# The low parts of one stage's weights, made a stage earlier and kept in DRAM

## The chip, the cores and the metric

One core of a Trainium2 chip runs the whole program. The metric is the time of one execution in device microseconds (us). TensorE (PE) multiplies, VectorE (DVE), ScalarE (ACT) and GpSimd (POOL) do the rest, and SyncE (SP) issues nearly all DMAs, in program order: a DMA that waits for a semaphore holds every DMA behind it on that engine.

## The reference

A trunk of two layers on 272 tokens (16 meta tokens and 256 of the input) of width 2048, in fp32. Each layer is a mixing part and a gated feed-forward; the mixing part of the second layer is an S5 scan beside an RWKV-7 recurrence:

```python
for layer in range(DEPTH):
    hn = rmsnorm(h, norm_mix_g[layer])
    if layer % 2 == 0:
        z = hn @ ev_w_in[j]          # LRU and differential attention
        ...
    else:
        z = hn @ od_w_in[j]          # 2048 x 4512
        u, dcols = z[..., :S5_WIDTH], z[..., S5_WIDTH:]
        yc = s5_layer(u, ...)        # then a gelu and a gated linear unit
        yd = rwkv7_time_mix(dcols, ...)
        mix = jnp.concatenate([yc, yd], axis=-1) @ od_w_out[j]
    h = h + mix
    h = h + swiglu(rmsnorm(h, norm_ffn_g[layer]), w_gate[layer], w_up[layer], w_down[layer])
```

## The kernel before

Activations lie with features on partitions and tokens along the row. Every dense product is exact to nearly fp32 by three passes: an operand is split into a high part that TensorE's fp32r format holds exactly and a low part, the rest, and `hi*xhi + hi*xlo + lo*xhi` is summed in PSUM (lines 193 to 195). A weight matrix is cut into pieces of 1024 x 128, 512 KB each. `load_piece_` loads a piece into `st`, casts it on ScalarE into `hi` (line 159) and subtracts on VectorE, `lo = st - hi` (line 160). `st`, `hi` and `lo` have three buffers each. A piece is 24 matmuls.

`run_dense` walks one list of items: the first mixing part, the first feed-forward (`ffn_items(0, ...)`), the second mixing part (`mix1_items`), the second feed-forward. An item is an output tile of 128 features: its pieces, where its input comes from, what to do with the result (`evac`), and what else to emit after it (`post`). Pieces are loaded a few ahead of use. `s5_setup` returns 15 steps that prepare tables for the S5 scan; they hang on every tenth item of the first feed-forward, the table steps at low priority, and the last one closes their pools. The tables go to DRAM (`s5p<-stb`, eight stores of 1088 KB) and come back as `stab` in the second mixing part.

In the second mixing part the items are the 36 tiles of `w_od_in`, two pieces each, in the order in which the scan (`s5_states`, from `us` and `stab`) and the recurrence (`rwkv`) need them; then the gated unit (`w_glu`) and the output product (`w_od_out`). `u` tiles are written to DRAM by `s5u<-zs` and `s5u<-ze` and read back as `us`. Scan and recurrence are long chains of small instructions over VectorE, ScalarE, GpSimd and TensorE. The order on each engine is made by the framework's scheduler when the program is built; priorities (`hi_pri` for weight loads) move instructions forward in it.

Of the kernel before, what the change touches and what calls it, by code (L numbers as in the profile page):

```python
# [9 lines left out]
F32 = mybir.dt.float32  # L10
F32R = mybir.dt.float32r
AF = mybir.ActivationFunctionType
ALU = mybir.AluOpType
# [81 lines left out]
class Net:  # L95
# [50 lines left out]
    def lo_pri(self):  # L146
        return self.tc.high_priority(offset=-1000000)

    def load_piece(self, ap, kc):
        with self.hi_pri():  # L150
            return self.load_piece_(ap, kc)

    def load_piece_(self, ap, kc):
        nc = self.nc
        st = self.t(self.wst, [128, 8, 128], "st")
        nc.sync.dma_start(st[:, :kc], ap)
        hi = self.t(self.whi, [128, 8, 128], "hi", F32R)
        lo = self.t(self.wlo, [128, 8, 128], "lo", F32R)
        nc.scalar.copy(hi[:, :kc], st[:, :kc])  # L159
        nc.vector.tensor_tensor(lo[:, :kc], st[:, :kc], hi[:, :kc].bitcast(F32), op=ALU.subtract)  # L160
        return hi, lo

    def run_dense(self, items, first=(), lead=0, ahead=2):

        nc = self.nc
        flat = [(i, j) for j in range(2) for i in range(lead)]
        flat += [(i, j) for i, it in enumerate(items) for j in range(len(it["pieces"])) if i >= lead]
        loads = [x for x in flat if items[x[0]]["pieces"][x[1]]]
        ready = dict(zip(loads, first))
        banks, done = {}, {}  # L170
        nxt, pos = len(first), 0
        for i, j in flat:
            it = items[i]
            if j == 0:
                if it.get("pre"):
                    it["pre"]()
                banks[i] = self.ps(it["bank"]) if "bank" in it else self.pd.tile([128, 512], F32, tag="p", name="p")
                done[i] = 0
            if it["pieces"][j]:
                while nxt < min(pos + 1 + ahead, len(loads)):  # L180
                    ready[loads[nxt]] = self.load_piece(*items[loads[nxt][0]]["pieces"][loads[nxt][1]])
                    nxt += 1
                pos += 1
                hi, lo = ready.pop((i, j))
            a, b, k0, c0, n = it["x"]()
            kc = it.get("kc") or it["pieces"][j][1]
            o = it.get("off", 0)
            tot = it.get("kc") or sum(kc for _, kc in it["pieces"])
            p = banks[i]
            for k in range(kc):  # L190
                kk = done[i]
                xa, xb = a[:, k0 + kk, c0:c0 + n], b[:, k0 + kk, c0:c0 + n]
                nc.tensor.matmul(p[:, :n], hi[:, o + k], xa, start=kk == 0, stop=False)  # L193
                nc.tensor.matmul(p[:, :n], hi[:, o + k], xb, start=False, stop=False)  # L194
                nc.tensor.matmul(p[:, :n], lo[:, o + k], xa, start=False, stop=kk == tot - 1)  # L195
                done[i] += 1
            if done[i] == tot:
                it["evac"](p[:, :n])
                if it.get("post"):
                    it["post"]()  # L200
# [385 lines left out]
    def s5_setup(self):  # L586

        nc = self.nc
# [3 lines left out]
        es = ExitStack()  # L592
        st = {}
# [100 lines left out]
        def weights_b():  # L694

            pl = st["plq"]
            bb = st["bb"]
            hm = self.s5c["hq"]
            eh = self.t(pl, [128, 8, 2, 2, 64], "seh", F32R)
            el = self.t(pl, [128, 8, 2, 2, 64], "sel", F32R)  # L700
            for g in range(2):
                m = hm[:, g:g + 1]
                nc.scalar.activation(eh[:, :, :, g], bb, AF.Copy, scale=m)
                V.scalar_tensor_tensor(el[:, :, :, g], bb, m, eh[:, :, :, g].bitcast(F32), op0=M, op1=S)
            par = self.s5_par.rearrange("(c s) p w -> s p c w", s=4)
            for i, x in enumerate((eh, eh, el, el)):
                for sc in range(4):
                    nc.sync.dma_start(par[sc, 32 * i:32 * i + 32, :, 2 * T:2 * T + 256],
                                      x[32 * sc:32 * sc + 32].rearrange("p c m g s -> p c (m g s)").bitcast(F32))
            st["es2"].close()  # L710
            st["pl2"] = self.pool("s5s2", 2, es)

        def weights_c(half):
            def f():
                cw = self.t(st["pl"], [128, 16, 3, 2, 16], "scw")
                for i, m in ((0, 0), (1, 1), (2, 1)):
                    for g in range(2):
                        sg = self.base["hm"][:, g:g + 1] if i < 2 else self.s5c["hn"][:, g:g + 1]
                        nc.scalar.activation(cw[:, :, i, g], st["c"][:, m, 16 * half:16 * half + 16], AF.Copy, scale=sg)
                nc.sync.dma_start(self.s5_par[16 * half:16 * half + 16, :, 2 * T + 256:].rearrange("j p c -> p j c"),  # L720
                                  cw.rearrange("p a i g c -> p a (i g c)"))
            return f
# [38 lines left out]
        def low(fn):  # L761
            def f():
                with self.lo_pri():
                    fn()
            return f

        steps = [scalars, factors, weights_b, weights_c(0), weights_c(1), small]
        steps += [low(table(g)) for g in range(8)]
        steps.append(es.close)
        return steps  # L770

    def s5_states(self, c, u, sc):
# [50 lines left out]
    def mix1_items(self):  # L823
        nc = self.nc
        I = self.I
        st = {}
        w, wo, wg = I["w_od_in"], I["w_od_out"], I["w_glu"]
        items = []
# [96 lines left out]
        def outp(last, m):  # L925
            def evac(p):
                self.add_h(p, m, NM)
                if last:
                    self.norm_chunk(m, "g_ffn1", NM)
                    if m == KC - 1:  # L930
                        st["es"].close()
            return evac

        def add(m, evac):
            items.append(dict(pieces=[(w[m, j], 8) for j in range(2)], x=x_in, evac=evac))

        for m, n in ((32, "w"), (33, "a"), (34, "g0"), (35, "g1")):
            add(m, lora(n, m - 8))
        add(0, u(0))
        for pr in range(8):  # L940
            for i in range(3):
                e = 3 * pr + i
                for c in range(1, 8):
                    if (4 * c * S5E + 31) // 32 - 1 == e:
                        add(c, u(c))
                add(8 + 8 * i + pr, rkv(pr, i))
# [13 lines left out]
        for m in range(KC):  # L960
            items.append(dict(pieces=[None if m % nb else (self.I["w_od_last"][m // nb], 8)], 
                              x=lambda: (*st["yd"], 0, 0, TR), kc=8 - YA, off=m % nb * (8 - YA), evac=outp(True, m)))
# [244 lines left out]
    def build(self, upto=99):  # L1207
        nc = self.nc
        with self.es:
            self.setup()  # L1210
            items = self.mix0_items()
            first = []
            with self.tc.high_priority(offset=100000):
                nc.sync.dma_start(self.vec, self.I["vec"])
            items[0].pop("pre")()
            with self.tc.high_priority(offset=100000):
                for a, b, i in ((0, 2, 1), (2, 8, 2), (8, 16, 0)):
                    nc.sync.dma_start(self.h[:, a:b], self.I["hT"][:, a:b])
                    for _ in range(i):
                        first.append(self.load_piece_(*items[len(first)]["pieces"][0]))  # L1220
                self.base = self.load_const("base", self.cp)
                self.mhalf = self.t(self.cp, [128, 8], "mhalf")
                nc.vector.memset(self.mhalf, -0.5)
                self.attn_setup()
                for k in range(KC):
                    self.norm_split(k, "g_mix0", 0)
            for k in range(KC):
                self.norm_square(k, 0, True)
            f0 = self.ffn_items(0, 0, None, lambda m: self.norm_chunk(m, "g_mix1", 0))
            steps = self.s5_setup()  # L1230
            for i, fn in enumerate(steps):
                f0[2 + 10 * i]["post"] = fn
            items += f0
            if upto > 1:
                items += self.mix1_items()
            if upto > 2:
                items += self.ffn_items(1, NM, None, self.final)
            self.run_dense(items, first, 3)
            if upto > 2:
                self.output()  # L1240
            if "h" in self.dbg:
                nc.sync.dma_start(self.dbg["h"], self.h)
# [95 lines left out]
```

## Time and profile before

| | |
|---|---|
| median of 3 runs | 2631.05 us (2630.87 to 2631.34) |
| the profiled execution | 2625.82 us, span 2624.0 us |
| TensorE busy | 2558.7 us, 98% of the span |
| VectorE, ScalarE, GpSimd busy | 1698.1, 1221.0, 591.2 us |
| mean granted TensorE clock | 0.989 of full speed |
| DMA | 448.37 MB, mean 171 GB/s |

The profile is one execution. Busy time is the time in which an engine executes; TensorE's is modelled and counts overlapping matmuls once. Positions are us from the start of the span: the first feed-forward runs from about 430 to 1225, the second mixing part to about 1850. The granted clock is the share of full TensorE speed (2.4 GHz) in a stretch; its lower level is 1.2 GHz.

### The profile page before, as it was taken

How to read it: one execution, taken by the hardware profiler on the slowest of the kernel's cores; microseconds unless marked ns; L12 is line 12 of the kernel's file. 1: busy time of each engine (PE TensorE's matmuls, PEld its weight loads, DVE VectorE, ACT ScalarE, POOL GpSimd, SP SyncE). 2: the span in 40 equal slices, each digit the busy share in tenths (PEclk: the TensorE clock that was granted, in tenths of full speed). 3: DMA queues.
4: the chain of work that ended last, by engine and by line, in shares of the span. 5: the costliest groups of instructions: out<-in, count | busy, mean ns of one | idle time of the engine just before them, and what ended most of it. 6: DMA issues, size and time to landing. Idle time of an engine off the chain costs nothing. (4 is left out here: it accounts for less than half of the span.)

```text
span 2624.0 us, 50534 instructions
## 1 busy us (share of the span) xinstructions
PE 2558.7 (98%) x20072; PEld 2467.8 (94%) x20072; DVE 1698.1 (65%) x2700; ACT 1221.0 (47%) x2111; POOL 591.2 (23%) x820
## 2 busy tenths in 40 slices
PE   8999999999999999999999999999999999999998
PEld 7999999999999999999877788899999999999997
DVE  7666768787555555557688898765655555555555
ACT  5555546488334333335334444554544434343434
POOL 3111312100001010102276777630210101010103
PEclk9999999999999999999999999999999999999999
DMA  5444456767655555555554444233555555555554
GB/s 193 145 141 139 145 180 199 223 221 243 204 176 176 172 176 175 172 176 180 176 163 150 140 143 128 87 117 124 175 186 179 187 186 185 188 185 185 185 185 145
DMA packets 160317, 448.37 MB, mean 171 GB/s; under 512 B 35089, under 2 KB 51153, under 8 KB 159825
## 3 DMA queue, kind: packets, MB, share of 16 engines
q1 hardware_dynamic: 143504, 442.84, 52.0%
q10 hardware_dynamic: 16576, 2.30, 0.5%
q8 instruction: 159, 2.61, 0.4%
q14 instruction: 78, 0.63, 0.1%
HBM read 422.20 MB, written 22.87 MB: 170 GB/s over the span
## 5 line engine op out<-in xcount | busy, mean ns | idle before, releaser
L159 ACT CAST hi<-st 128x1024 fp32r<-128x1024 f32 (+1 forms) x776 | 792.9, 1022 | 1074.5 <-PE p L194 770.0
L160 DVE TENSOR_TENSOR lo<-st,hi 128x1024 fp32r<-128x1024 f32 (+1 forms) x776 | 936.4, 1207 | 489.8 <-ACT hi L159 485.8
L193 PE MATMUL p<-xhi,hi 128*128 128x272 f32 (+1 forms) x4256 | 1233.5, 290 | 12.4 <-ACT hi L159 10.0
L195 PE MATMUL p<-xhi,lo 128*128 128x272 f32 (+1 forms) x4256 | 1236.5, 291 | 7.0 <-DVE lo L160 6.9
L194 PE MATMUL p<-xlo,hi 128*128 128x272 f32 (+1 forms) x4256 | 1229.6, 289 | 0.0
L193 PEld LDWEIGHTS p<-xhi,hi 128*128 128x128 f32 x4256 | 809.1, 190 | 25.7 <-issue 12.9
L195 PEld LDWEIGHTS p<-xhi,lo 128*128 128x128 f32 x4256 | 809.0, 190 | 20.8 <-issue 11.2
L194 PEld LDWEIGHTS p<-xlo,hi 128*128 128x128 f32 x4256 | 807.6, 190 | 10.8 <-issue 10.0
L299 POOL TENSOR_TENSOR ga<-ga,rb 128x272 f32<-128x272 f32 (+1 forms) x88 | 126.1, 1433 | 1231.5 <-ACT ga L298 1231.5
L195 PE MATMUL p<-ah,lo 128*128 128x272 f32 (+1 forms) x1408 | 401.9, 285 | 0.4 <-DVE lo L160 0.4
L193 PE MATMUL p<-ah,hi 128*128 128x272 f32 (+1 forms) x1408 | 401.0, 285 | 0.3 <-ACT hi L159 0.3
L194 PE MATMUL p<-al,hi 128*128 128x272 f32 (+1 forms) x1408 | 400.9, 285 | 0.0
L195 PEld LDWEIGHTS p<-ah,lo 128*128 128x128 f32 x1408 | 265.8, 189 | 0.7 <-DVE lo L160 0.7
L193 PEld LDWEIGHTS p<-ah,hi 128*128 128x128 f32 x1408 | 265.6, 189 | 0.6 <-ACT hi L159 0.6
L194 PEld LDWEIGHTS p<-al,hi 128*128 128x128 f32 x1408 | 264.8, 188 | 0.0
L208 DVE TENSOR_TENSOR h<-p,h 128x256 f32<-128x256 f32 (+1 forms) x272 | 116.8, 430 | 145.1 <-PE p L195 144.1
L245 POOL TENSOR_TENSOR acc<-acc,sq 128x272 f32<-128x272 f32 (+1 forms) x56 | 60.7, 1084 | 260.0 <-ACT sq L240 259.5
L308 DVE TENSOR_TENSOR gu<-p,ga 128x272 f32<-128x272 f32 (+1 forms) x88 | 38.1, 433 | 62.4 <-PE p L195 59.9
L297 DVE TENSOR_TENSOR ga<-p,rb 128x272 f32<-128x272 f32 (+1 forms) x88 | 38.0, 432 | 53.4 <-PE p L195 52.8
L806 POOL TENSOR_TENSOR sx<-stab,sz 128x256 f32<-128x256 f32 x64 | 63.5, 995 | 27.6 <-DVE sz L803 10.5
L1096 POOL TENSOR_TENSOR xt<-ls,xs 40x15 f32<-40x15 f32 (+7 forms) x120 | 49.9, 416 | 43.8 <-DMA ls<-ld 37.4
L218 DVE SCALAR_TENSOR_TENSOR xlo<-h,vec,xhi 128x272 fp32r<-128x272 f32 (+1 forms) x64 | 50.7, 800 | 0.6 <-ACT xhi L217 0.5
(383 smaller groups left out, 2594.4 us busy)
## 6 DMA issues: line engine op xcount, KB each, us to landing
st<-in_w_gate SPq DMA_DIRECT2D x176, 512.0 KB
st<-in_w_up SPq DMA_DIRECT2D x176, 512.0 KB
st<-in_w_down SPq DMA_DIRECT2D x160, 512.0 KB
st<-in_w_ev_in SPq DMA_DIRECT2D x80, 512.0 KB
st<-in_w_od_in SPq DMA_DIRECT2D x72, 512.0 KB
st<-in_w_ev_out SPq DMA_DIRECT2D x32, 512.0 KB
stab<-s5p SPq DMA_DIRECT2D x32, 448.0 KB
s5p<-stb SPq DMA_DIRECT2D x8, 1088.0 KB
```

The source lines that it names most:

```text
L159: nc.scalar.copy(hi[:, :kc], st[:, :kc])
L160: nc.vector.tensor_tensor(lo[:, :kc], st[:, :kc], hi[:, :kc].bitcast(F32), op=ALU.subtract)
L193: nc.tensor.matmul(p[:, :n], hi[:, o + k], xa, start=kk == 0, stop=False)
L194: nc.tensor.matmul(p[:, :n], hi[:, o + k], xb, start=False, stop=False)
L195: nc.tensor.matmul(p[:, :n], lo[:, o + k], xa, start=False, stop=kk == tot - 1)
L208: self.nc.vector.tensor_tensor(self.h[:, m, c0:], p, self.h[:, m, c0:], op=ALU.add)
L218: nc.vector.scalar_tensor_tensor(lo, src, g, hi.bitcast(F32), op0=ALU.mult, op1=ALU.subtract)
L245: nc.gpsimd.tensor_tensor(self.acc[:, c0:], self.acc[:, c0:], sq[:, c0:], op=ALU.add)
L299: nc.gpsimd.tensor_tensor(a[:, :n], a[:, :n], self.rb[:, :n], op=ALU.mult)
L308: nc.vector.tensor_tensor(u[:, :n], p, a[:, :n], op=ALU.mult)
L806: (V if i == 3 else G).tensor_tensor(pr[i], a[:, NM:], b[:, NM:], op=M)
L1096: G.tensor_tensor(o, ls[:, s + 1:, s].unsqueeze(1).to_broadcast([40, j, n]), xs[:, :j, s:s + 1].to_broadcast([40, j, n]), op=M)
```

## The change

The low parts of the 72 pieces of `w_od_in` are no longer made when the pieces are used. A new function `park` loads a piece into `pst`, casts it into `phi`, subtracts in place and stores the result to a DRAM tensor `od_lo`; 72 calls of it hang on items of the first feed-forward from item 24 on, spread evenly by pieces. In the second mixing part such a piece's `hi` is cast as before, and its `lo` is loaded from DRAM. The S5 pools are closed near the end of the feed-forward instead of at item 142, since the two double-buffered tiles of `park` live among them. The scratch space that the framework keeps for dynamic DMAs is set to 1024.

```diff
-    def load_piece_(self, ap, kc):
+    def load_piece_(self, ap, kc, parked=None):
...
         nc.scalar.copy(hi[:, :kc], st[:, :kc])
-        nc.vector.tensor_tensor(lo[:, :kc], st[:, :kc], hi[:, :kc].bitcast(F32), op=ALU.subtract)
+        if parked is None:
+            nc.vector.tensor_tensor(lo[:, :kc], st[:, :kc], hi[:, :kc].bitcast(F32), op=ALU.subtract)
+        else:
+            nc.sync.dma_start(lo.bitcast(F32), parked)
         return hi, lo
+
+    def park(self, pl, ap, parked):
+        nc = self.nc
+        st = self.t(pl, [128, 8, 128], "pst")
+        nc.sync.dma_start(st, ap)
+        hi = self.t(pl, [128, 8, 128], "phi", F32R)
+        nc.scalar.copy(hi, st)
+        nc.vector.tensor_tensor(st, st, hi.bitcast(F32), op=ALU.subtract)
+        nc.sync.dma_start(parked, st)
...
             st["pl2"] = self.pool("s5s2", 2, es)
+            self.park_pool = self.pool("park", 2, es)
...
-            items.append(dict(pieces=[(w[m, j], 8) for j in range(2)], x=x_in, evac=evac))
+            items.append(dict(pieces=[(w[m, j], 8, self.od_lo[m, j]) for j in range(2)], x=x_in, evac=evac))
...
+            first_, todo, at = 24, list(parts), 0.0
+            each = sum(size[first_:-4]) / len(parts)
+            for i in range(first_, len(f0) - 4):
+                at += size[i]
+                while todo and at >= each:
+                    at -= each
+                    posts[i].append(lambda x=todo.pop(0): self.park(self.park_pool, x[0], x[2]))
...
+            posts[-2].append(lambda: self.s5_pools.close())
...
-    nc = bacc.Bacc("TRN2", target_bir_lowering=False, num_devices=1)
+    nc = bacc.Bacc("TRN2", target_bir_lowering=False, num_devices=1, dynamic_dma_scratch_size=1024)
```

The scheduler places what this emits. Three places are shown, each before and after; line numbers of the changed program are its own (its 156 is the weight load, 161 the subtraction, 163 the load of `lo`, 170 to 174 the park).

SP in the first feed-forward, between its gate and up products and the down product of a slice. Before, there are weight loads alone:

```order
L156 DMA st<-in_w_gate 128x1024 x2
L156 DMA st<-in_w_up 128x1024 x2
L156 DMA st<-in_w_gate 128x1024 x2
L156 DMA st<-in_w_up 128x1024 x2
L156 DMA st<-in_w_down 128x1024 x32
```

After, with the semaphores that each row waits for (`DVE_49` is VectorE's, `DMAHWn_49` those of earlier DMAs, which is how a park's load waits for the store that frees its buffer):

```order
L156 DMA st<-in_w_gate 128x1024 [waits DMAHW5_49,DVE_49]
L170 DMA pst<-in_w_od_in 128x1024 [waits DMAHW3_49,DMAHW0_49]
L156 DMA st<-in_w_up 128x1024 [waits DMAHW6_49,DVE_49]
L174 DMA odlo<-pst 128x1024 [waits DVE_49]
L156 DMA st<-in_w_up 128x1024 [waits DMAHW1_49,DVE_49]
L156 DMA st<-in_w_down 128x1024 [waits DMAHW7_49,DMAHW2_49,DVE_49]
L170 DMA pst<-in_w_od_in 128x1024 [waits DMAHW5_49]
L174 DMA odlo<-pst 128x1024 [waits DVE_49]
L156 DMA st<-in_w_down 128x1024 [waits DMAHW4_49,DVE_49]
L156 DMA st<-in_w_down 128x1024 [waits DMAHW6_49,DMAHW3_49,DVE_49]
```

For every two or three weight loads there is now one park's load and one store, each with a wait of its own. All 72 stand between the 145th and the 314th weight load of the program.

SP at the start of the second mixing part. Before (the first rows of its weight loads):

```order
L156 DMA st<-in_w_od_in 128x1024 [waits DMAHW6_49,DVE_49]
L156 DMA st<-in_w_od_in 128x1024 [waits DMAHW7_49,DVE_49]
L133 DMA c_rw<-in_c_rw 128x912 [waits PE_49]
L978 DMA lw<-in_w_lora 128x256 [waits Pool_49]
L980 DMA lg<-in_w_lora 128x256
L156 DMA st<-in_w_od_in 128x1024 [waits DMAHW0_49,DVE_49]
```

After:

```order
L163 DMA lo<-odlo 128x1024 [waits PE_49]
L156 DMA st<-in_w_od_in 128x1024 [waits DMAHW6_49,Activation_49]
L163 DMA lo<-odlo 128x1024 [waits PE_49]
L156 DMA st<-in_w_od_in 128x1024 [waits DMAHW7_49,Activation_49]
L163 DMA lo<-odlo 128x1024 [waits PE_49]
L133 DMA c_rw<-in_c_rw 128x912
L994 DMA lw<-in_w_lora 128x256 [waits Pool_49]
L156 DMA st<-in_w_od_in 128x1024 [waits DMAHW0_49,Activation_49]
```

Weight loads and `lo` loads now alternate. A `lo` load waits for TensorE to release the buffer (`PE_49`), a weight load for the cast (`Activation_49`) instead of the subtraction.

VectorE inside the second mixing part, where scan (`sx`, `sz`, `sp`), recurrence (`rkv`, `lz`) and weights share it. Before:

```order
L802 SCALAR_TENSOR_TENSOR sz_15205<-s_rho,sx_15191 128x272
L160 TENSOR_TENSOR lo<-st,hi 128x1024
L806 TENSOR_TENSOR sp_15212<-stab,sz_15205 128x256
L803 SCALAR_TENSOR_TENSOR sz_15206<-s_rho,sx_15192 128x272
L1059 TENSOR_TENSOR lz<-a,c_rw 128x64
L1059 TENSOR_TENSOR lz<-a,c_rw 128x2x64
L792 TENSOR_TENSOR sx_15302<-c,stab 128x272
L793 TENSOR_TENSOR sx_15303<-c,stab 128x272
L204 TENSOR_TENSOR zs<-p,rb 128x272
L160 TENSOR_TENSOR lo<-st,hi 128x1024
```

After:

```order
L816 SCALAR_TENSOR_TENSOR sz_15753<-s_rho,sx_15739 128x272
L820 TENSOR_TENSOR sp_15760<-stab,sz_15753 128x256
L1048 TENSOR_TENSOR ri_14967<-rkv_16225,rcu 128x4x64
L817 SCALAR_TENSOR_TENSOR sz_15754<-s_rho,sx_15740 128x272
L217 TENSOR_TENSOR zs<-p,rb 128x272
L806 TENSOR_TENSOR sx_15773<-c,stab 128x272
L807 TENSOR_TENSOR sx_15774<-c,stab 128x272
```

The subtractions of input weights are gone from between the scans; the rest stands in a new order. On TensorE the first matmul that reads `us` (line 791) comes 325 dense matmuls after the last one of the norm's broadcast (line 269), where it came after 248.

## Rows read from the trace of the kernel before

**Rows 1.** The page's first lines: span, and busy time by engine.

```profile
span 2624.0 us, 50534 instructions
PE 2558.7 (98%) x20072; PEld 2467.8 (94%) x20072; DVE 1698.1 (65%) x2700; ACT 1221.0 (47%) x2111; POOL 591.2 (23%) x820
```

**Rows 2.** Busy time by stretch, with clock and DMA.

```profile
core 0: us, PE busy (x) PEld busy (x) DVE busy (x) ACT busy (x) POOL busy (x), PEclk, DMA share, GB/s
1260.00:1290.00 30.00, 25.95 (x184) 25.76 (x183) 15.98 (x24) 8.39 (x10) 5.25 (x9) 0.89 0.56 175
1290.00:1640.00 350.00, 337.62 (x2285) 278.39 (x2283) 294.87 (x464) 149.77 (x308) 249.12 (x425) 0.99 0.47 147
1640.00:1730.00 90.00, 82.34 (x611) 73.28 (x610) 67.19 (x123) 49.20 (x115) 54.08 (x100) 0.96 0.30 91
440.00:700.00 260.00, 252.38 (x1950) 250.12 (x1949) 194.04 (x358) 162.05 (x387) 25.64 (x21) 0.98 0.68 222
700.00:1200.00 500.00, 500.00 (x3967) 500.00 (x3967) 266.43 (x312) 193.19 (x224) 39.58 (x28) 1.00 0.53 174
```

**Rows 3.** Waits of TensorE, 1260 to 1730: us in total, times, longest.

```profile
PE a L1202 <- DVE re L1199: 5.9, 4, 2.4
PE d L807 <- POOL sx L806: 4.1, 3, 2.8
PE c L791 <- DMA us<-s5u: 4.0, 1, 4.0
PE e L1157 <- DVE w L1154: 2.4, 1, 2.4
...
```

**Rows 4.** Timeline around one gap: start, us, engine, line, instruction.

```profile
1364.06 1.19 DVE L160 TENSOR_TENSOR lo<-st,hi 128x1024 fp32r<-128x1024 f32 x1
1365.18 0.95 DVE L1199 COPY re<-iv 68x512 f32<-68x512 f32 x1
...
1366.28 0.30 PE L1202 MATMUL a<-c_base,re 68*128 68x68 f32 x1 [2.45 <-DVE re L1199]
```

**Rows 5.** Chain of waits, 1260 to 1730: the subtractions before 1640 on it.

```profile
1511.87 1.58 DVE lo L160
...
1533.61 1.19 DVE lo L160
...
1611.84 1.21 DVE lo L160
```

**Rows 6.** Line 160 from 1260 to 1730: min, median and max ns.

```profile
L160 DVE TENSOR_TENSOR lo<-st,hi x72: 1191/1224/1808, 1259.7 to 1726.0; 128x1024 fp32r<-128x1024 f32 x72
```

**Rows 7.** Line 156 from 1250 to 1800: the loads of `w_od_in`.

```profile
L156 SPq DMA_DIRECT2D st<-in_w_od_in x61: 327/333/634, 1251.9 to 1623.5; - x61
```

**Rows 8.** Waits of ScalarE, 700 to 1200; the 166 casts there.

```profile
ACT hi L159 <- PE p L194: 221.4, 113, 2.0
ACT hi L159 <- issue: 84.8, 52, 1.9
...
L159 ACT CAST hi<-st x166: 1047/1051/1053, 699.8 to 1199.1; 128x1024 fp32r<-128x1024 f32 x166
```

**Rows 9.** Waits of SP, 700 to 1200.

```profile
SPq L156 <- DVE lo L160: 368.9, 141, 2.9
```

**Rows 10.** Timeline of SP and ScalarE from 593: loads issued, casts that waited.

```profile
593.40 1.32 SPq L156 DMA_DIRECT2D st<-in_w_gate  x2
595.39 4.16 SPq L156 DMA_DIRECT2D st<-in_w_up  x2
...
596.88 1.05 ACT L159 CAST hi<-st 128x1024 fp32r<-128x1024 f32 x1 [0.47 <-DMA st<-in_w_gate]
599.26 1.05 ACT L159 CAST hi<-st 128x1024 fp32r<-128x1024 f32 x1 [0.50 <-DMA st<-in_w_gate]
601.88 1.05 ACT L159 CAST hi<-st 128x1024 fp32r<-128x1024 f32 x1 [1.57 <-DMA st<-in_w_up]
```

**Rows 11.** Timeline: a table's store, and what waited for it.

```profile
585.04 0.43 SPq L757 DMA_DIRECT2D s5p<-stb  x1
...
590.61 0.30 DVE L747 COPY stb<-stq 128x256 f32<-128x256 f32 x1 [0.77 <-DMA s5p<-stb]
```

**Rows 12.** Timeline of TensorE: the first matmul that reads `us`.

```profile
1276.98 0.57 PE L791 MATMUL c<-us,stab 128*128 128x272 f32 x1 [4.05 <-DMA us<-s5u]
```

**Rows 13.** The page's DMA lines: queue, packets, MB, share; issues.

```profile
q1 hardware_dynamic: 143504, 442.84, 52.0%
...
st<-in_w_od_in SPq DMA_DIRECT2D x72, 512.0 KB
...
s5p<-stb SPq DMA_DIRECT2D x8, 1088.0 KB
```

**Rows 14.** Busy time in one microsecond.

```profile
604.00:605.00 1.00, 1.00 (x11) 1.00 (x10) 0.82 (x4) 1.00 (x3) 0.00 (x0) 1.00 1.06 418
```

More of the change, by code (lines that the diff above doesn't have):

```diff
@@ L147, in lo_pri, with load_piece @@
         return self.tc.high_priority(offset=-1000000)
-    def load_piece(self, ap, kc):
+    def load_piece(self, *piece):
         with self.hi_pri():
-            return self.load_piece_(ap, kc)
-    def load_piece_(self, ap, kc):
+            return self.load_piece_(*piece)
+    def load_piece_(self, ap, kc, parked=None):
         nc = self.nc
@@ L187, in run_dense @@
             o = it.get("off", 0)
-            tot = it.get("kc") or sum(kc for _, kc in it["pieces"])
+            tot = it.get("kc") or sum(x[1] for x in it["pieces"])
             p = banks[i]
@@ L765, in low @@
             return f
+        self.s5_pools = es
         steps = [scalars, factors, weights_b, weights_c(0), weights_c(1), small]
         steps += [low(table(g)) for g in range(8)]
-        steps.append(es.close)
         return steps
@@ L932, in outp @@
             return evac
+        self.od_lo = self.dr.tile([36, 2, 128, 8, 128], F32, tag="odlo", name="odlo")
         def add(m, evac):
-            items.append(dict(pieces=[(w[m, j], 8) for j in range(2)], x=x_in, evac=evac))
+            items.append(dict(pieces=[(w[m, j], 8, self.od_lo[m, j]) for j in range(2)], x=x_in, evac=evac))
         for m, n in ((32, "w"), (33, "a"), (34, "g0"), (35, "g1")):
@@ L1229, in build @@
             f0 = self.ffn_items(0, 0, None, lambda m: self.norm_chunk(m, "g_mix1", 0))
-            steps = self.s5_setup()
-            for i, fn in enumerate(steps):
-                f0[2 + 10 * i]["post"] = fn
+            m1 = self.mix1_items()
+            posts = [[] for _ in f0]
+            for i, fn in enumerate(self.s5_setup()):
+                posts[2 + 10 * i].append(fn)
+            parts = [x for it in m1 for x in it["pieces"] if x and len(x) == 3]
+            size = [sum(x[1] for x in it["pieces"]) for it in f0]
+            first_, todo, at = 24, list(parts), 0.0
[5 more added lines that the diff above has]
+                    posts[i].append(lambda x=todo.pop(0): self.park(self.park_pool, x[0], x[2]))
+            for x in todo:
+                posts[-5].append(lambda x=x: self.park(self.park_pool, x[0], x[2]))
+            posts[-2].append(lambda: self.s5_pools.close())
+            for it, fns in zip(f0, posts):
+                if fns:
+                    it["post"] = lambda fns=fns: [f() for f in fns]
             items += f0
-            if upto > 1:
-                items += self.mix1_items()
+            items += m1
             if upto > 2:
```

## The prediction

> **What bounds the kernel now.** I read the page first, then busy time by stage, then who TensorE waited for. The profiled execution took 2625.82 us around a span of 2624.0 us; the median of the runs is 2631.05, so every difference worked out below in the profile's microseconds is put on 2631.05, and the 0.2% between the two is passed over. TensorE is busy 2558.7 us of the span [rows 1]: what can be won is the 65 us in which it is idle, and what its clock loses after such a gap. By stage [rows 2] the reader should see three different kernels. In the first feed-forward from 700 to 1200 us TensorE has 500 of 500 us, VectorE 266 and ScalarE 193: nothing there can be won, and there is room to hide work. From 440 to 700 us, where the feed-forward shares its engines with the preparation of the S5 tables, TensorE is idle 7.6 us and VectorE and ScalarE are fuller (194 and 162 of 260). In the second mixing stage TensorE is idle 4.05 us in 1260 to 1290, 12.38 in 1290 to 1640 and 7.66 in 1640 to 1730, and VectorE is the fullest of the others, 294.87 of 350 us (84%). The granted clock of these three stretches is 0.89, 0.99 and 0.96 of full speed; the missing share is worth 3.3, 3.5 and 3.6 us at 2.4 GHz.
>
> The waits [rows 3] name VectorE or GpSimd behind most of this idle time, and one DMA: the first `us` load, 4.0 us. One gap shows the mechanism that the change aims at [rows 4]: TensorE waits 2.45 us for `re` of line 1199, and VectorE had run a 1.19 us subtraction of line 160 right before it. In the chain of waits the subtraction of input weights stands three times with 1.58, 1.19 and 1.21 us [rows 5]. That chain reaches back only to 1487 us.
>
> **The change, part by part.** (1) *Removed.* 72 subtractions go from VectorE in the second mixing stage. One takes 1.22 us [rows 6], so 88 us in all, some 66 of them in 1290 to 1640, where VectorE falls from 84% to about 65%. What that gives TensorE lies between 1.1 us (the one gap of [rows 4], in which the subtraction stood directly ahead) and 12.4 us (all idle time of 1290 to 1640; the last of these 72 pieces is loaded at 1623.5, [rows 7]). The nearest row is the chain: 3.98 us in the 153 us from 1487 to 1640, so 9.9 us over the 380 us from 1260. I take 10, and of the 3.5 us that the clock loses there the same share, 3.
>
> (2) *A moved start.* The order shows that in the new program 325 dense matmuls instead of 248 stand between the last matmul of the norm (line 269) and the first that needs `us`. At 0.126 us each (500 us for 3967 [rows 2]) this is 9.7 us more time for that load. Bounds: nothing, if the load is late by as much, since the new `lo` loads stand in the same queue; 7.3 us, if the gap and its clock loss both go (4.05 + 3.3). I take 4.
>
> (3) *Added in the first feed-forward*, 72 times: a 512 KB load, a ScalarE cast of 1.05 us, a VectorE subtraction of 1.22 us and a 512 KB store. Casts and subtractions come to 76 and 88 us. The cover is the slack of 700 to 1200 us: ScalarE waits there for TensorE to release `hi` [rows 8], 306 us over 166 casts, 1.8 us in each period of 3.02 us (24 matmuls of 0.126), and VectorE is 53% busy. Engine time costs nothing there. Without that cover, as in part of 440 to 700 us, a park is 2.3 us on the way to the next `hi` and `lo`.
>
> The queue is the doubtful part. SP issues in order. Before, it sits in front of each weight load waiting for VectorE, 369 us over 141 loads, 2.6 us of 3.02 [rows 9]. Now a store that waits for its subtraction, or a park load that waits until its buffer's store has landed, holds the weight loads behind it, and those hold TensorE. By the order, 170 weight loads (154 of 512 KB, 16 of 256 KB) stand between the first park's load and the last one's store: 162 periods of 3.02 us, 490 us, so a park every 6.8 us and, with two buffers, 13.6 us for one round of load, cast, subtraction and store. What a round needs: a 512 KB load lands 3.5 us after issue when it is alone (593.40 to 596.88) and 4.9 us when one is ahead [rows 10]; a cast waits up to 2.0 us for its turn behind a `hi` cast and takes 1.05, the subtraction 1.22 and up to as much for its turn; the store takes 3.5 us if like a load, 5.6 if like the `stb` store of 1088 KB (585.04 to 590.61) [rows 11]. Low end 9.3, high end 16.0, middle 12.6 us. With 12.6 the rounds fit, tightly. I take 4 us for moments where they don't, above all before 700 us; bounds 0 and 85 us ((16.0 - 13.6) / 2 times 72).
>
> (4) *Added in the second mixing stage:* 72 loads of 512 KB into `lo`. A `lo` load can be issued when TensorE has finished the piece three before, two pieces ahead of its use. In the first 20 pieces hardly anything stands between the dense matmuls, so that is 6.05 us; later, 380 us for some 60 pieces makes it about 12.6. A load with two others in flight lands after 6.5 us (595.39 to 601.88) [rows 10], so in the long run it is in time, and in the first 20 pieces it may be late by up to 0.44 us, 9 us in all. The `s5u` stores, the first of which holds `us` back until 1276.98 [rows 3, 12], stand in the same queue and can add to it. I take 4 us; bounds 0 and 61 (a landing of 9.1 us, one more transfer of 2.6 us ahead, is late by 3.0 in each of 20 pieces).
>
> (5) *Moved and freed.* The S5 pools are closed at the end of the feed-forward instead of at its item 142; what takes their place begins only after that feed-forward, so this costs nothing. In the mixing stage an `st` buffer is now free after the cast, 1.2 us earlier than after the subtraction: nothing won, since the weight loads have been early enough there (of the waits of [rows 3] none is for `st`). The smaller scratch space carries no instruction of the profile.
>
> The sum: -10 - 3 - 4 + 0 + 4 + 4 = -9 us, from 2631 to **2622 us**.
>
> **The rivals.** *No difference.* In 1290 to 1640 TensorE is 96% busy; if the gaps only move to the next late engine (GpSimd is at 71%, 249 of 350), the gain is the 1.1 us of the one gap, or what is won is given back in (3) and (4). For it: the waits in [rows 3] run through GpSimd's `iv` and `sx` as well as VectorE. Time 2626 to 2636.
>
> *The parks become the bound of the feed-forward* (the other side). Transfers in that stretch: 154 x 512 + 16 x 256 KB of weights, 72 x 1024 KB of parks and 8 x 1088 KB of tables, 169.3 MB in 490 us, 345 GB/s. Over the whole span queue 1 moved 442.84 MB in 52.0% of the time of 16 engines [rows 13], which is 325 GB/s at full occupancy. At that rate the stretch takes 522 us: +32. With the gains and the cost of (4), -13, it gives 2650; if rounds of 16.0 us decide, +85 and 2703. Against it: with a store and a load in flight together, single microseconds show 418 GB/s [rows 14], and sustained at that rate 405 us would do. It decides from a round of 13.6 us, or below 345 GB/s. The Trainium skill (DMA: Bandwidth & Descriptors, section Specifications) gives a limit of about 358 GB/s of HBM for one core and 435 GB/s for the engines. By the former the 169.3 MB would take 473 us, so this rival would cost nothing on average. The rate of [rows 14] is beyond 358, so the trace does not bear that limit out for single microseconds, and no row shows 345 held for 490 us.
>
> *`lo` comes late at the start of the mixing stage.* If a landing takes 7.0 us in place of 6.05, 20 pieces lose 19 us, against gains of 17 and the 4 us of (3): 2637. It speaks for it that the same stretch asks for 1 MB every 3.02 us, 347 GB/s, with the `s5u` stores between.
>
> *More than forecast.* All idle time of 1290 to 1730 outside the DMA gap goes (20.0), the clock follows (7.1) and so does the first gap (7.3), at no cost: -34, 2597.
>
> **How the numbers follow.** The forecast, 2610 to 2625, has 0.40; more than that, down to 2597, 0.12; no difference 0.19; the parks as bound 0.16; late `lo` 0.13. A measurement of this kernel can tell about 0.2% (5.3 us) from no change. Faster by more than that takes the first two, 0.52; within it 0.19; slower 0.29. The range leaves out the far half of the parks' rival and little at the low end: 2597 to 2655. Without the two slower cases it would be 2600 to 2633.
>
> **What would show it.** Right: in the stretch that is now 1290 to 1640, VectorE near 65% busy, TensorE's idle time near 3 us, no wait of line 195's matmuls for a DMA named `lo<-odlo` beyond the first 20 pieces, and 500 of 500 us busy in the feed-forward with DMA at some 345 GB/s. Wrong: ScalarE waiting for `st` or `pst` loads in the feed-forward and TensorE idle behind `hi`, with the clock below 1.00 there (the parks); TensorE waiting for `odlo` (late `lo`); or the same idle time in the mixing stage with other releasers, GpSimd first (no difference).

## The result, and the profile after

The changed kernel takes 2650.91 us (median of 5 runs, 2644.98 to 2657.92) against 2631.05 before: ratio 1.0074, 95% interval 1.0052 to 1.0095. It is slower by 20 us, where 9 us faster was forecast. The time lies within the range and on the other side of no change; it is the time that the rival "the parks become the bound of the feed-forward" gave (2650). The profiled execution took 2652.13 us.

The page of the kernel after, its first lines and its chain of waits, to be read beside [rows 1]:

```profile
span 2650.3 us, 50949 instructions
PE 2568.2 (97%) x20072; PEld 2471.8 (93%) x20072; DVE 1688.5 (64%) x2700; ACT 1293.3 (49%) x2183; POOL 552.5 (21%) x820
...
PE 71%; DMA 14%; DVE 6%; issue 3%; ACT 3%; POOL 2%; SPq 1%; ACTq 0%; DVEq 0%; POOLq 0%
```

The totals say little: all engines have about the work they had, ScalarE 72 us more. Only the chain of waits (third line) points somewhere: DMA has 14% of it. The stretches, with the columns of [rows 2], say where:

```profile
440.00:700.00 260.00, 239.79 (x1788) 233.76 (x1787) 208.34 (x371) 175.42 (x399) 27.32 (x17) 0.97 0.85 297
700.00:1200.00 500.00, 495.48 (x3901) 492.37 (x3900) 309.05 (x350) 236.84 (x264) 37.57 (x28) 1.00 0.81 277
...
1290.00:1670.00 380.00, 367.17 (x2527) 311.31 (x2525) 236.43 (x422) 163.04 (x325) 218.95 (x446) 0.97 0.71 234
1670.00:1760.00 90.00, 84.31 (x600) 73.51 (x600) 69.13 (x126) 47.24 (x113) 55.62 (x103) 0.96 0.29 83
```

The number behind each x counts matmuls, and in the feed-forward all are alike, so the difference to [rows 2] is TensorE's lag, idle time and slow clock together. From 440 to 700 us there are 1788 in place of 1950, 162 fewer, 20.4 us at 0.126 us each. From 700 to 1200 there are 3901 in place of 3967, 66 fewer, 8.3 us. That makes 28.7 us lost in the first feed-forward. The issue of the first mixing piece's load agrees, 1216.59 us before and 1246.92 after, 30.3 us later.

The mixing stage does get its VectorE relief: 236 of 380 us (62%) in 1290 to 1670, where it was 84%. TensorE gets little of it. Over 700 us of that stage it is idle 29.0 us before (1200 to 1900, busy 671.02) and 25.2 after (1230 to 1930, busy 674.82).

Waits of ScalarE, 500 to 1250 us, in the kernel after (us in total, times, longest):

```profile
ACT hi L159 <- PE p L207: 122.9, 76, 2.0
ACT phi L172 <- DMA pst<-in_w_od_in: 84.6, 43, 4.0
ACT hi L159 <- issue: 28.6, 18, 1.7
ACT hi L159 <- DMA st<-in_w_down: 25.0, 22, 3.1
ACT hi L159 <- DMA st<-in_w_gate: 23.2, 24, 2.2
```

Waits of SP in the same stretch:

```profile
SPq L156 <- DVE lo L161: 256.4, 134, 3.5
SPq L170 <- DMA odlo<-pst: 107.1, 52, 4.6
...
SPq L174 <- DVE pst L173: 39.3, 37, 5.0
```

Before, ScalarE waited there for TensorE and had time in hand [rows 8]. Now it waits for weights on their way, and 43 times for a parking load at the head of its own order. SP stands 107 us before parking loads until the buffer's store has landed. TensorE's own waits, 440 to 700 us, are for weights (in the kernel before they were 3.4 and 4.1 us in the same stretch):

```profile
PE p L206 <- ACT hi L159: 10.9, 8, 3.4
PE p L208 <- DVE lo L161: 9.1, 11, 2.5
```

This is what the prediction named as the sign of the rival. The waits show two candidates and not which of them costs the time: too many bytes, or waiting instructions at the head of an order.

### The profile page after: what moved, and what is told of

The parts are those of the page before. It is cut to its first block, busy times and chain, and to the rows that moved or that the text cites. A ratio compares the mean times of both kernels' runs of the same rounds, so it can differ in the third digit from the quotient of the medians.

```text
span 2650.3 us, 50949 instructions
## 1 busy us (share of the span) xinstructions
PE 2568.2 (97%) x20072; PEld 2471.8 (93%) x20072; DVE 1688.5 (64%) x2700; ACT 1293.3 (49%) x2183; POOL 552.5 (21%) x820
## 4 chain that ended last, share of the span: by engine, by line
PE 71%; DMA 14%; DVE 6%; issue 3%; ACT 3%; POOL 2%; SPq 1%; ACTq 0%; DVEq 0%; POOLq 0%
PE p L208 21%; PE p L206 21%; PE p L207 21%; DMA odlo<-pst 5%; DMA pst<-in_w_od_in 4%; PE d L821 2%; DVE lo L161 2%; DMA st<-in_w_gate 1%; DMA lo<-odlo 1%; ACT hi L159 1%; DVE pst L173 1%; ACT phi L172 1%; DMA st<-in_w_down 1%; PE b L1139 1%; POOL xs L1114 1%
## 5 line engine op out<-in xcount | busy, mean ns | idle before, releaser
L161 DVE TENSOR_TENSOR lo<-st,hi 128x1024 fp32r<-128x1024 f32 (+1 forms) x704 | 842.7, 1198 | 410.3 <-ACT hi L159 404.1
L173 DVE TENSOR_TENSOR pst<-pst,phi 128x1024 f32<-128x1024 f32 x72 | 89.1, 1237 | 69.2 <-ACT phi L172 67.8
L172 ACT CAST phi<-pst 128x1024 fp32r<-128x1024 f32 x72 | 75.4, 1047 | 85.1 <-DMA pst<-in_w_od_in 84.6
L820 POOL TENSOR_TENSOR sx<-stab,sz 128x256 f32<-128x256 f32 x64 | 54.6, 855 | 28.8 <-DVE sz L817 11.1
```

The costliest lines, as they stand in the source:

```text
L172: nc.scalar.copy(hi, st)
L173: nc.vector.tensor_tensor(st, st, hi.bitcast(F32), op=ALU.subtract)
L820: (V if i == 3 else G).tensor_tensor(pr[i], a[:, NM:], b[:, NM:], op=M)
```

## The experiments

"Lag" is the matmuls missing against [rows 2] in 440 to 700 and in 700 to 1200 us, times 0.126 us. "Rest" is the difference of the medians less both lags: what the other stages, mostly the mixing stage, win (-) or lose. The lags come from one profiled execution each, in which some matmul records can be missing, and the late parks still run after 1200 us; the three kernels without loads in the mixing stage have rests of 4.2, -0.7 and 2.8, so a rest is good to some 4 us. Each kernel was timed beside the kernel before on the same chip (medians 2630.38, 2629.42 and 2630.02 in the three groups of four).

| kernel | median us | ratio (95%) | lag 440–700 | lag 700–1200 | rest |
|---|---|---|---|---|---|
| changed kernel | 2650.91 | 1.0074 (1.0052–1.0095) | 20.4 | 8.3 | -8.8 |
| parks only | 2657.94 | 1.0101 (1.0086–1.0117) | 18.5 | 4.9 | 4.2 |
| loads only | 2617.96 | 0.9949 (0.9934–0.9965) | -2.0 | 0 | -10.4 |
| parks, transfers only | 2660.36 | 1.0119 (1.0101–1.0137) | 26.7 | 4.0 | -0.7 |
| parks, engines only | 2635.27 | 1.0020 (1.0008–1.0031) | 2.1 | 0 | 2.8 |
| paced | 2634.77 | 1.0019 (1.0006–1.0033) | 3.4 | 9.3 | -7.4 |
| paced, late | 2644.19 | 1.0055 (1.0037–1.0073) | -1.8 | 18.8 | -2.2 |
| parks on GpSimd's queue | 2681.45 | 1.0198 (1.0179–1.0218) | 26.1 | 27.6 | -1.7 |
| paced, late, four `lo` | 2657.86 | 1.0104 (1.0086–1.0122) | -2.4 | 19.4 | 11.4 |
| staged, late | 2625.31 | 0.9990 (0.9980–1.0000) | -0.8 | 1.1 | -5.0 |
| half of the parks | 2634.46 | 1.0025 (1.0012–1.0038) | 15.8 | 0 | -11.4 |
| staged | 2623.56 | 0.9980 (0.9971–0.9988) | 3.2 | 0 | -9.7 |
| staged, late, half | 2618.30 | 0.9961 (0.9948–0.9974) | -1.1 | 0 | -10.6 |

**Which half of the change costs.** Parks only: the mixing stage keeps its subtractions.

```diff
-        if parked is None:
+        if True:
             nc.vector.tensor_tensor(lo[:, :kc], st[:, :kc], hi[:, :kc].bitcast(F32), op=ALU.subtract)
```

> The 72 parks of the first feed-forward are as in the changed kernel, but the mixing stage computes its low parts by subtraction as before, and nothing reads what was parked. If the loss lies in the first feed-forward (theory A, from the trace of after: first mixing piece reached 30 us later, the stage itself only 3 us shorter), this costs 26 to 32 us over the kernel before, about 2660, and is slower than the changed kernel by about 3 to 10. If the loss came from the stage that loads the parked parts (theory B), it is within 6 us of before, 2631 to 2637.

Loads only: one piece is parked, and all 72 loads read that place.

```diff
-                    posts[i].append(lambda x=todo.pop(0): self.park(self.park_pool, x[0], x[2]))
+                    x = todo.pop(0)
+                    if x is parts[0]:
+                        posts[i].append(lambda x=x: self.park(self.park_pool, x[0], x[2]))
...
-            nc.sync.dma_start(lo.bitcast(F32), parked)
+            nc.sync.dma_start(lo.bitcast(F32), self.od_lo[32, 0])
```

> One piece is parked, and all 72 low parts of the mixing stage are loaded from that one place, so the low parts are not the reference's. This is the mixing stage of the changed kernel without the traffic in the feed-forward. Theory A: 3 to 13 us faster than before, 2618 to 2628 (13 is what the prediction gave this stage, 3 is what the trace of after shows). Theory B: 20 us or more slower than before.

2657.94 and 2617.96: theory A twice (the second at the edge of its range), B falls. Parking costs 27.6 us, loading wins 12.4. Together they give +15.2, and the changed kernel has +19.9, with an interval of 13.7 to 25.0 us: the difference is within the noise.

**Transfers or engine work.** Both keep the subtractions of the mixing stage. Transfers only, in `park`:

```diff
-        hi = self.t(pl, [128, 8, 128], "phi", F32R)
-        nc.scalar.copy(hi, st)
-        nc.vector.tensor_tensor(st, st, hi.bitcast(F32), op=ALU.subtract)
```

> Parks without cast and subtraction: each piece is loaded and stored again as it is, and the mixing stage subtracts as before. A1 (the feed-forward loses because its transfers need more than the roughly 325 GB/s that the DMA moves at full occupancy): nearly all the loss stays, 20 to 30 us over before, about 2656. A2 (it loses because parking casts and subtractions stand in ScalarE's and VectorE's order waiting for the parking load, and hold up the weights' casts behind them): under 8 us over before, 2631 to 2639.

Engines only, in `park`, where `st` is one tile that is set once:

```diff
-        nc.sync.dma_start(st, ap)
...
-        nc.sync.dma_start(parked, st)
```

> Parks without transfers: the 72 casts and 72 subtractions run on one tile that is in place, and the mixing stage subtracts as before. A1: within 4 us of before, 2628 to 2636. A2: the same, since nothing waits. A3 (the loss is the engine time itself, 150 us of ScalarE and VectorE together, most of it at 550 to 660 us where both engines are already at 42 of 50 us): 10 to 25 us over before, 2641 to 2656.

2660.36 and 2635.27. The transfers alone bring all of the loss, 30 us, and A2 falls; the engine work alone brings 4.9, and A3 falls. The first is not quite the transfers of the changed kernel: without casts the 72 parks run closer together, from 511.2 to 968.1 us (457 us) where the changed kernel takes 522. But the stretches of the kernel with transfers only do not fit a plain ceiling:

```profile
500.00:600.00 100.00, 86.07 (x622) 83.39 (x621) 70.59 (x155) 76.48 (x229) 6.29 (x6) 0.95 0.94 340
600.00:700.00 100.00, 92.61 (x674) 89.44 (x674) 55.83 (x94) 51.62 (x114) 6.84 (x6) 0.95 0.97 351
700.00:800.00 100.00, 100.00 (x786) 98.97 (x785) 51.21 (x63) 38.12 (x43) 3.88 (x4) 1.00 0.96 341
800.00:900.00 100.00, 99.74 (x779) 98.33 (x779) 49.11 (x60) 37.71 (x45) 4.66 (x6) 1.00 0.96 340
```

At nearly the same rate and share (340 GB/s, 0.94 to 0.97), TensorE is idle 13.9 us at 500 to 600 us (4.6 before), and its clock is 0.95. At 700 to 900 it is idle 0.3 us, and 25 matmuls are missing against the 795 of each 100 us before, 3.2 us. The difference, as far as these numbers tell, is what the kernel itself needs there: 230 GB/s before 700 us, where the tables are stored and 16 weight pieces are half-sized, 174 after it [rows 2]. What the transfers of 500 to 600 us are, in the kernel before and then in the kernel after (issues, KB each):

```profile
DMA packets 9634, 23.03 MB, mean 230 GB/s; under 512 B 811, under 2 KB 2462, under 8 KB 9624
...
st<-in_w_gate SPq DMA_DIRECT2D x12, 512.0 KB
st<-in_w_up SPq DMA_DIRECT2D x12, 512.0 KB
...
st<-in_w_down SPq DMA_DIRECT2D x16, 256.0 KB
```

```profile
DMA packets 12300, 32.87 MB, mean 329 GB/s; under 512 B 1091, under 2 KB 2952, under 8 KB 12291
...
pst<-in_w_od_in SPq DMA_DIRECT2D x12, 512.0 KB
odlo<-pst SPq DMA_DIRECT2D x11, 512.0 KB
st<-in_w_gate SPq DMA_DIRECT2D x10, 512.0 KB
st<-in_w_up SPq DMA_DIRECT2D x10, 512.0 KB
...
st<-in_w_down SPq DMA_DIRECT2D x14, 256.0 KB
```

Parks take 23 x 0.524 MB = 12.1 of the 32.9 MB. Weights fall from 16.8 to 14.2 MB, by 16%, and TensorE's matmuls follow: from 726 to 661 in these 100 us, from 790 to 679 in the next. In SP's order, which the scheduler made, a park's load and store stand behind every two or three weight loads, so the parks take their share of the transfers whether or not the weights can spare it.

**Pace, place and queue.** The source hangs the parks on items of nearly the whole feed-forward; the scheduler's order has them run ahead, and in the trace of after the last one's store is issued at 1034.0 us, 213 us before the mixing stage's first load. So in the next kernels each load waits for the product that it follows; the late one also gives the first 28% of the stretch 0.4 of the rate. `self.last` is one column of that product's result.

```diff
         st = self.t(pl, [128, 8, 128], "pst")
+        nc.vector.tensor_copy(st[:, 0, :1], self.last)
         nc.sync.dma_start(st, ap)
...
-                at += size[i]
+                run += size[i]
+                at += size[i] * (0.4 if run < 0.28 * total else 1.0)
```

The other two: the parks of the changed kernel, not paced, on GpSimd's queue; and the paced, late kernel with four buffers for `lo`.

```diff
-        nc.sync.dma_start(st, ap)
+        nc.gpsimd.dma_start(st, ap)
...
-        nc.sync.dma_start(parked, st)
+        nc.gpsimd.dma_start(parked, st)
...
-        self.wlo = self.pool("wlo", 3)
+        self.wlo = self.pool("wlo", 4)
```

> The changed kernel, but each parking load waits for the product that its place in the program follows (one element of that product's result is copied into the buffer first), so parks are spread over the whole feed-forward, one per about 9.9 us, where the trace of after has them run ahead and end at 1050 us. A1a (the loss is a ceiling of the transfers, met because parks ran ahead at the pace that two buffers allow): 500 to 700 us then ask 232 + 106 = 338 GB/s, at the upper end of the 317 to 338 that after reached, and lose up to 8 us; later stretches ask 174 + 106 = 280 and lose nothing; with the 12 us of the loads alone the time is 2618 to 2628. A1b (the loss is that weight loads stand behind parking transfers which wait in SP's order, 107 us for stores and 39 us for subtractions in after): as many parks still wait, so half or more of the loss stays, 2636 to 2650.

> As the paced kernel, but with 0.4 of the parks' rate in the first 28% of the stretch, where the state-space tables are made. A1a: 232 + 50 = 282 GB/s up to 700 us and about 295 after it, both below what after reached, so nothing is lost to transfers: 2615 to 2623. A1b: 2636 to 2650, as the paced one.

> The changed kernel with the parks' loads and stores issued by GpSimd on its own queue, so no weight load stands behind a waiting park; the pace of the parks is left free. A1a: the same bytes run ahead at the same stretch, so the loss stays: 2643 to 2656. A1b: the loss goes, 2618 to 2628.

> As the paced and late kernel, with four buffers for low parts in place of three. If the waits of TensorE for a loaded low part (8.3 us in four waits after) come from a buffer that is free too late, this takes most of them: 3 to 8 us faster than the paced and late one, 2609 to 2618. If they come from transfers already queued, no difference, 2615 to 2623.

2634.77, 2644.19, 2681.45 and 2657.86: neither theory holds throughout (only the second lies in a range given for it, that of A1b). Pacing takes the early loss away as A1a said (20.4 to 3.4 and to nothing), but a later one has grown, from 8.3 to 9.3 and 18.8, at transfers of 287 and 294 GB/s. Where it begins is in ScalarE's waits, here of the paced kernel, 700 to 1200 us:

```profile
ACT phi L173 <- DMA pst<-in_w_od_in: 115.3, 55, 4.1
ACT hi L159 <- PE p L208: 100.5, 62, 3.0
```

A parking cast stands at the head of ScalarE's order 2.1 us on average until its load lands, and the weights' casts behind it wait too. What reaches TensorE comes through VectorE: its parking subtraction (line 174) stands at the head in its turn, and behind that the addition to `h` (line 222), which TensorE waits for before its next product. TensorE's waits in the same stretch, VectorE's, and the longest gap as a timeline:

```profile
PE p L207 <- DVE h L222: 6.0, 6, 2.1
DVE pst L174 <- ACT phi L173: 102.8, 52, 3.9
...
1000.64 1.05 ACT L173 CAST phi<-pst 128x1024 fp32r<-128x1024 f32 x1 [3.26 <-DMA pst<-in_w_od_in]
1001.72 1.23 DVE L174 TENSOR_TENSOR pst<-pst,phi 128x1024 f32<-128x1024 f32 x1 [3.05 <-ACT phi L173]
1002.86 0.43 DVE L222 TENSOR_TENSOR h<-p,h 128x272 f32<-128x272 f32 x1
...
1003.44 0.36 PE L207 MATMUL p<-ah,hi 128*128 128x272 f32 x1 [2.11 <-DVE h L222]
```

The three longest gaps (2.1, 1.7 and 1.2 us, of 6.9 us idle in all) have this form. On GpSimd's queue no weight load stands behind a park, yet the early loss stays (26.1), which is against A1b, and the later one is the largest of all (27.6). Waits of GpSimd and ScalarE there, 500 to 1250 us:

```profile
POOL pst L170 <- DMA odlo<-pst: 196.1, 53, 10.3
...
ACT phi L172 <- DMA pst<-in_w_od_in: 109.5, 47, 6.2
...
POOL odlo L174 <- DVE pst L173: 98.9, 26, 9.1
```

GpSimd's own work now stands behind waiting transfers, but the trace shows no engine waiting for GpSimd in this stretch; ScalarE's waits for parking loads have grown from 84.6 to 109.5 us. Which of these makes the later loss is not shown.

The fourth `lo` buffer takes away nearly all waits of TensorE for `odlo` (5.9 us in the paced, late kernel, 0.5 with it), and the kernel is 13.7 us slower than that one, against both expectations. Its clock is 0.90 and 0.91 in 1600 to 1700 and 1700 to 1800 us, where the other has 0.97 in both. Why the stage as a whole went worse stays open.

**Two losses.** This gave theory C, with a kernel that takes both away. A park becomes three stages, each a park later than the one before, with load and cast tied to a product; the subtraction writes into the cast's buffer, and that is stored. In `park`, with `q` the list of parks under way and `self.last` now a column of the product in its bank:

```diff
+        if len(q) > 1 or ap is None:
+            hi, to = q.pop(0)
+            nc.sync.dma_start(to, hi.bitcast(F32))
+        if q:
+            st, to = q.pop(0)
+            hi = self.t(pl, [128, 8, 128], "phi", F32R)
+            nc.vector.tensor_copy(hi[:, 0, :1], self.last)
+            nc.scalar.copy(hi, st)
+            nc.vector.tensor_tensor(hi.bitcast(F32), st, hi.bitcast(F32), op=ALU.subtract)
+            q.append((hi, to))
```

The late ones begin at product 60, and the halves park every second piece:

```diff
-            first_, todo, at = 24, list(parts), 0.0
+            first_, todo, at = 60, list(parts), 0.0
...
-            items.append(dict(pieces=[(w[m, j], 8, self.od_lo[m, j]) for j in range(2)], x=x_in, evac=evac))
+            items.append(dict(pieces=[(w[m, 0], 8, self.od_lo[m, 0]), (w[m, 1], 8)], x=x_in, evac=evac))
```

> Parks in three stages, each tied to a later product (load; one park later cast and subtraction; one park later the store, from the cast's buffer), and none before the state-space tables are done, so about 7 us apart from 690 us on. Theory C (two losses: transfers at their ceiling while the tables are made, about 22 us in after, and casts and subtractions that wait for a parking load at the head of ScalarE's and VectorE's order, about 10 us after 750 us): both are gone, the rate asked is 174 + 144 = 318 GB/s, which the parks without casts held at 340 with TensorE fully busy; 2616 to 2626, faster than before. Theory D (each parked piece costs about 0.3 to 0.4 us of TensorE wherever it stands): 2640 to 2650, as the paced kernels.

> The same three stages, but spread from 590 us on, about 9.9 us apart, so that some 11 parks share the stretch of the tables. Theory C: 0 to 8 us more than the staged and late one, 2618 to 2632, and under the paced kernel (2634.8). Theory D: as the paced one, 2632 to 2640.

> The staged and late kernel with every second piece of the mixing stage parked (36) and the others subtracted as before. Theory C: nothing lost in the feed-forward, half of the 12 us of the loads won: 2622 to 2627. Theory D: 36 x 0.35 = 13 lost, 6 won, 2634 to 2640.

> The changed kernel as it is, with every second piece parked, so parks run ahead from 505 us and end near 780. Theory C: the loss in the stretch of the tables stays whole (20 to 22), little behind it (2), half of the 12 us won: 2642 to 2650, no better than the changed kernel by more than a few us. Theory D: half the loss and half the gain, 2637 to 2641.

2625.31, 2623.56, 2618.30 and 2634.46: the first three below the kernel before (the first by an interval that ends at 1.0000), against theory D. The first two lie in theory C's ranges, the third is 4 us faster than its range, since the half won 10.6 and not 6. The feed-forward of the staged, late kernel, in two stretches:

```profile
440.00:700.00 260.00, 252.72 (x1956) 250.64 (x1955) 194.14 (x361) 163.40 (x387) 31.75 (x19) 0.98 0.68 221
700.00:1200.00 500.00, 499.05 (x3958) 498.86 (x3957) 357.76 (x514) 256.51 (x290) 38.07 (x27) 1.00 0.90 315
```

and the waits of its ScalarE, 700 to 1200 us:

```profile
ACT hi L159 <- PE p L217: 217.4, 138, 2.0
...
ACT phi L177 <- DMA pst<-in_w_od_in: 3.8, 2, 3.2
```

All 72 parks, 315 GB/s, and a lag of 1.1 us: more bytes per us than the paced kernels moved at 287 to 294, where 9 and 19 us went. The wait of parking casts has fallen from 115.3 to 3.8 us, and ScalarE waits for TensorE again, as in [rows 8]. Staging changed SP's order too, but SP still stands 149 us before the parks' loads and stores here, 186 in the paced kernel (700 to 1200 us), so that wait alone does not make the 9 us. With some 12 parks before 700 us (the staged one) 3.2 us are lost there and none after it.

Half of the parks, run as in the changed kernel, missed: the early loss is smaller than the whole (15.8 of 20.4) and the rest wins 11.4 in place of 6, so it came out below both ranges, 2.5 us under theory D's. Its stretches are theory C's (all of its lag before 700 us, 3967 matmuls after it). The staged, late half beats both kernels: 2618.30, ratio 0.9961 (0.9948 to 0.9974).

## Why the prediction was wrong

**The step that failed is (3), in its term for the queue:** "With 12.6 the rounds fit, tightly. I take 4 us for moments where they don't". It measured 23.4 us of lag with the parks alone and 28.7 in the whole change, within the bounds of 0 and 85. Two assumptions in it were wrong.

- It tested rounds against the mean of the whole stretch, one park every 6.8 us. The order puts one park behind every two or three weight loads, whatever the stretch can spare. Where the kernel needs 230 GB/s and parks add 121 (23 transfers in 100 us), the DMA moved 329 of the 351, and the weights got less. That is 20 of the 28.7 us, before 700 us. This loss stays without casts (26.7 us with transfers only) and without a weight load behind a park in SP's order (26.1 on GpSimd's queue), and it goes when few parks stand there (paced, late: none lost). By elimination it is the bytes.
- "Engine time costs nothing there" is right of the engine time (casts and subtractions alone: lag 0 after 700 us). But an instruction that waits for a load also holds its engine's order. In the paced kernel the three longest gaps, 5.0 us of a lag of 9.3, come that way, and with the staged parks 1.1 us of lag is left. In the changed kernel it is at most a part of the other 8 us, since the transfers alone leave 4.0 of lag there; the split was not measured. (Of the 306 us that (3) counts as ScalarE waiting for TensorE, 84.8 are "issue" in [rows 8], for which the profile names no releaser.)

The rival came out at the right time, 2650, and half by the right mechanism. From the first park's load to the last one's store the changed kernel took 522 us (512.4 to 1034.0) at 324 GB/s, just what the rival said, and it priced the stage at +32, where 28.7 are measured. But 325 GB/s is not the most that the DMA moves: the kernel with transfers only holds 340 to 351 over stretches of 100 us, and 315 cost 1.1 us when hardly anything waited at the head of an order. Nor is the loss even over the stretch, as a bound by rate alone would have it: 20 of the 28.7 us come before 700 us. What decides is how much of the rate is left to the weights. The Trainium skill (DMA: Bandwidth & Descriptors, section Specifications) gives about 358 GB/s of HBM for one core; no stretch of 100 us here exceeds it, the highest found being 354 (535 to 635 us, transfers only). By that rule alone the parks would cost nothing, and they cost 20 us while under it.

**(1) and (2), the gain,** were of the right size: with the 4 us of (4) taken off they gave 13, and the loads alone win 12.4 (95% of the ratio: 9.2 to 17.4 of 2630). VectorE fell to 62%, 65 forecast. The trace explains only a part of it: TensorE's idle time over 700 us falls from 29.0 to 26.2 us with the loads alone, not by 10. The wait for the first `us`, 4.0 us in [rows 3], is gone, as (2) said. In 1290 to 1640 us the idle time falls from 12.4 to 6.5 us, not to the 3 that the prediction named as its sign, and in 1640 to 1730 it rises from 7.7 to 11.1, with GpSimd's `xs` and ScalarE's `mk` the longest waits there, 3.1 us each. In this execution, then, 17.6 of the 20.0 us of 1290 to 1730 are still idle, in other places and behind other engines, as the rival "no difference" had it. The medians confirm the size of the gain; the path to it is shown only in part. The profiled execution of before (2625.82 us) was itself 5.2 us below the median of its runs, and that with the loads alone (2619.89) 1.9 above; which idle time the other runs of before had more is not seen. In the changed kernel the rest wins 8.8 by the medians.

**(4)** had the right place of its waits and half their size. TensorE, 1210 to 1920 us, in the kernel after:

```profile
PE p L208 <- DMA lo<-odlo: 8.3, 4, 3.3
...
```

8.3 us in four waits, where 4 were taken and 9 held possible for the first 20 pieces. With half of the low parts loaded these waits are 3.1 us (staged, late, half), and the rest wins as much as with all, 10.6. So the second half of the parks bought nothing that the rests, good to some 4 us, can show.

**(5)** was not tested by itself.

## What to carry to other kernels

Work moved into a stage with idle engines must be priced by what it leaves to others at its busiest moment, not by the mean of the stage: ask of each stretch what the transfers need already, and what the new ones will take when nothing paces them. An instruction that waits for a load holds its engine's whole order, and other engines' behind it, so issue the load one step ahead of the work that reads it. And move only as much as the receiving stage can use: here half the pieces won as much as all, as far as the noise lets one see.

## What was not expected of the hardware

- A DMA share near 1 did not tell whether TensorE loses: at 0.94 and 329 GB/s the parks got 12.1 of 32.9 MB while TensorE lagged behind for weights, and at 0.96 and 341 GB/s (transfers only, 700 to 800 us) it was busy 100 of 100 us, with 786 matmuls where the kernel before has 795.
- An issue of a 512 KB transfer took 0.54 us on GpSimd (72 loads: 537 to 782 ns) and 0.33 us on SP (327 to 1397), and with the parks on GpSimd's queue 20736 packets of it carried 75.51 MB in 36.1% of the 16 engines' time of 500 to 1100 us. That is 349 GB/s at full occupancy, no slower per byte than SP's (105.89 MB in 49.8%, 354). So the queue's rate does not explain what that kernel lost.
